# Norm sums of the last two channel blocks in one accumulation group per PSUM bank, with later identity products and a halved first output piece

## The chip, the cores and the metric

The kernel runs on one core of a Trainium2 chip. The metric is the device time of one execution in microseconds (us); lower is better.

## The reference

One inference step through one layer of a decoder trunk, for a prompt of 256 tokens and for 8 samples of one token each, with `D_MODEL = 2048`. What matters here is the end of each of its two sub-layers: an output projection, a root-mean-square norm over the 2048 channels of each token, and a residual sum.

```python
def rmsnorm(x, g):
    xf = x.astype(jnp.float32)
    y = xf * lax.rsqrt(jnp.mean(xf * xf, axis=-1, keepdims=True) + EPS)
    return (y * g.astype(jnp.float32)).astype(x.dtype)

def trunk(x, c, s_hg, s_gla, p):
    # ... three token mixers, merged by gates ...
    out = merged @ p['w_out'][l]                                          # 2048 -> 2048
    x = x + gt1 * rmsnorm(out, p['g_post_mix'][l])
    h2 = rmsnorm(x, p['g_pre_mlp'][l]) * (1.0 + sc2) + sh2
    y2 = jnp.square(jax.nn.relu(h2 @ p['w_mlp_up'][l])) @ p['w_mlp_down'][l]  # 2048 -> 8192 -> 2048
    x = x + gt2 * rmsnorm(y2, p['g_post_mlp'][l])
```

The results are `y_prompt` (256 tokens by 2048 channels), `y_sample` (8 by 2048), the states of two recurrences and one set of gate rows.

## The kernel before

**Layout and products.** Activations are kept with channels on the 128 partitions and tokens along the free axis: 256 prompt tokens and 8 samples, 264 columns. Every large weight is streamed from HBM in tiles, split into a rounded part `whi` (on ScalarE) and a remainder `wlo` (on VectorE), and multiplied in three products per tile (lines 603 to 605). These products fill nearly the whole program. `w_out` and `w_mlp_down` give 16 output blocks of 128 channels each. Blocks 0 to 13 are made in pairs; the last two, 14 and 15, are made one after the other by code of their own, so that work on block 14 can run while TensorE multiplies for block 15.

**The norm sums.** For each block the squares of its 264 columns are added into `sqacc` (128 partitions by 264). The sum over the partitions is a product with ones on TensorE. For the prompt, the 128 columns of a token half `t` are the stationary operand and one column of ones moves, which leaves one sum per token on the partitions, in column `t` of a PSUM tile `ps`; for the samples, the ones are stationary and 8 columns move, which leaves their sums in columns 2 to 9. The squares of block 15 are not added to `sqacc`: they stay in `sq[:, 1, :]`, and each sum is a group of two products, one with `sqacc` and one with `sq[:, 1, :]`. This stands twice: after `w_out` (lines 1672 to 1676) and after `w_mlp_down` (lines 1941 to 1945). Squares and sums are in float32, and each float32 product shows in the trace as two passes on TensorE.

**After `w_out`.** From `ps` come the factors `r1` (a square root on ScalarE, line 1684, and a Newton step on VectorE, lines 1687 to 1695), then those of the next norm, `r2`, then two sets of scaled identity matrices (lines 1718 to 1722), and with these the first input blocks of `w_mlp_up` (`first_quad`, line 1750). While ScalarE and VectorE do this, TensorE works off 40 products of the conditioning matrix (`rounds.steps`, lines 1681 and 1699, the products at line 338).

**After `w_mlp_down`, the tail.** `rstd_sqrt` (lines 190 to 199) makes `r3` from `ps`: one square root on ScalarE and five short operations on VectorE. The output `y = x1 + r3 * yt` has 8 pieces of 128 tokens by 512 channels (`put`, line 1962). VectorE makes five of them (line 1968), and SyncE (SP) issues their transfers. TensorE makes the three in `by_pe`: an identity product that puts `x1` into PSUM (`first_part`, line 1926) and a product with a diagonal matrix of `r3` that adds the scaled rows (line 1973); ScalarE copies the sum out (line 1966) and issues the transfer itself. `rows_tile(1)` (line 1921) turns block 15 to token rows, which ScalarE then copies (line 1953). GpSimd scales the sample rows (lines 1959 and 1960), TensorE transposes them (line 1976), ScalarE copies them (line 1986) and SP issues the last transfer (line 1987).

The order of work on TensorE, VectorE and ScalarE is the order in which the code is written in these two places (`tc.manual_schedule`), so a line moved in the source is moved on its engine. The small PSUM tiles come from a pool of three buffers (`sm`).

## Time and profile before

| | |
|---|---|
| Runs | 1922.57, 4265.69 and 1923.81 us, median 1923.81 |
| Profiled execution | 1922.67 us, of which the span of the instructions is 1920.9 us |
| TensorE clock granted in it | 0.997 of full |
| TensorE busy | 1898.7 us in 17108 instructions |
| VectorE, ScalarE, GpSimd busy | 1201.5, 1007.6 and 156.8 us |
| HBM traffic | 435.99 MB read, 11.70 MB written |

The profile gives, for one execution, when each instruction began, how long it took, what ended the idle time before it, and which chain of work ended last. PE is TensorE's matmul, PEld its weight load, DVE is VectorE, ACT ScalarE, POOL GpSimd; SPq and ACTq are the queues from which SP and ScalarE issue transfers. Times count from the start of the span. A row of the timeline has start, duration, engine, line, operation, the names of output and inputs, shapes and a count of merged instructions; in brackets stand the idle time before it and what ended it.

### The profile page before, as it was taken

How to read it: one execution, taken by the hardware profiler on the slowest of the kernel's cores; microseconds unless marked ns; L12 is line 12 of the kernel's file. 1: busy time of each engine (PE TensorE's matmuls, PEld its weight loads, DVE VectorE, ACT ScalarE, POOL GpSimd, SP SyncE). 2: the span in 40 equal slices, each digit the busy share in tenths (PEclk: the TensorE clock that was granted, in tenths of full speed). 3: DMA queues.
4: the chain of work that ended last, by engine and by line, in shares of the span. 5: the costliest groups of instructions: out<-in, count | busy, mean ns of one | idle time of the engine just before them, and what ended most of it. 6: DMA issues, size and time to landing. Idle time of an engine off the chain costs nothing.

```text
span 1920.9 us, 42626 instructions
## 1 busy us (share of the span) xinstructions
PE 1898.7 (99%) x17108; PEld 1811.6 (94%) x17108; DVE 1201.5 (63%) x2139; ACT 1007.6 (52%) x1821; POOL 156.8 (8%) x314
## 2 busy tenths in 40 slices
PE   7999999999999999999999999999999999999998
PEld 5899999989999999999999989999999999999997
DVE  5666567685576694555555666555766666665666
ACT  4444454655755764544444565555555545454544
POOL 1000000100100101000000010121212121210000
PEclk8999999999999999999999999999999999999999
DMA  9996686776776777767787846797867776866553
GB/s 330 342 329 244 227 304 207 230 230 201 224 244 199 227 233 249 243 205 251 255 265 230 295 146 188 253 306 221 250 211 246 222 250 214 251 206 187 182 180 107
DMA packets 342455, 450.48 MB, mean 235 GB/s; under 512 B 15522, under 2 KB 281520, under 8 KB 342256
## 3 DMA queue, kind: packets, MB, share of 16 engines
q1 hardware_dynamic: 330000, 409.95, 66.2%
q0 software_dynamic: 11648, 36.94, 6.1%
q8 instruction: 134, 2.20, 0.5%
q10 hardware_dynamic: 608, 0.86, 0.1%
q14 instruction: 65, 0.53, 0.1%
HBM read 435.99 MB, written 11.70 MB: 233 GB/s over the span
## 4 chain that ended last, share of the span: by engine, by line
PE 97%; DMA 2%; DVE 1%; ACT 1%; issue 0%; SPq 0%; ACTq 0%
PE mm L603 29%; PE mm L604 29%; PE mm L605 29%; PE ada L338 3%; PE ada L270 1%; PE sm L653 1%; DMA raw<-in_w_in_dram 1%; PE sm L887 1%; DMA b<-in_w_ada_dram 1%; PE sm L660 1%; DVE wlo L107 0%; DMA b<-in_x_prompt_dram 0%; PE sm L994 0%; PE sm L1340 0%; PE sm L1295 0%; PE sm L1320 0%
## 5 line engine op out<-in xcount | busy, mean ns | idle before, releaser
L603 PE MATMUL mm<-b,whi 128*128 128x264 f32 x4568 | 1310.1, 287 | 4.3 <-DVE b L859 1.9
L604 PE MATMUL mm<-b,whi 128*128 128x264 f32 x4568 | 1298.9, 284 | 1.0 <-DVE b L107 0.9
L605 PE MATMUL mm<-b,wlo 128*128 128x264 f32 x4568 | 1296.4, 284 | 0.0
L107 DVE TENSOR_TENSOR wlo<-raw,whi 128x512 fp32r<-128x512 f32 x1136 | 775.4, 690 | 517.1 <-ACT whi L110 513.1
L110 ACT CAST whi<-raw 128x512 fp32r<-128x512 f32 x1132 | 696.3, 618 | 736.2 <-PE mm L604 672.6
L603 PEld LDWEIGHTS mm<-b,whi 128*128 128x128 f32 x4568 | 859.2, 188 | 46.2 <-issue 28.6
L604 PEld LDWEIGHTS mm<-b,whi 128*128 128x128 f32 x4568 | 859.8, 188 | 1.7 <-DVE b L107 0.7
L605 PEld LDWEIGHTS mm<-b,wlo 128*128 128x128 f32 x4568 | 859.3, 188 | 0.0
L104 DVE TENSOR_TENSOR b<-b,mm 128x528 f32<-128x528 f32 (+1 forms) x137 | 95.8, 700 | 95.0 <-PE mm L605 92.5
L1383 ACT ACTIVATE st<-st,sx 128x128 f32<-128x128 f32 (+1 forms) x96 | 39.2, 433 | 37.3 <-POOL sx L1380 37.3
L1384 DVE SCALAR_TENSOR_TENSOR st<-vbc,sx,st 128x128 f32<-128x128 f32 (+1 forms) x96 | 36.1, 394 | 28.8 <-ACT st L1383 28.8
L1362 POOL COPY sa<-vt 128x1 f32<-128x1 f32 x24 | 16.8, 699 | 297.4 <-ACT vt L1828 297.4
L338 PE MATMUL ada<-araw,cT 128*32 128x512 f32 x296 | 40.3, 601 | 0.0
L270 PE MATMUL ada<-b,cT 128*32 128x256 f32 (+1 forms) x640 | 34.6, 352 | 3.4 <-ACT b L234 2.7
L101 DVE TENSOR_TENSOR b<-b,b 128x512 f32<-128x512 f32 (+1 forms) x47 | 33.9, 741 | 1.7 <-ACT b L1262 0.9
L1362 POOL COPY sa<-b 128x1 f32<-128x1 f32 x42 | 18.9, 451 | 178.5 <-DVE b L104 142.0
L270 PEld LDWEIGHTS ada<-b,cT 128*32 128x32 f32 x640 | 17.8, 113 | 15.2 <-DMA b<-in_w_ada_dram 3.4
L338 PE MATMUL ada<-b,cT 128*32 128x512 f32 x216 | 25.8, 593 | 0.0
L107 DVE TENSOR_TENSOR b<-gt,b 128x528 fp32r<-128x528 f32 x32 | 22.7, 708 | 3.3
L107 DVE TENSOR_TENSOR b<-b 128x1024 f32<-128x1024 f32 (+1 forms) x24 | 24.3, 1016 | 0.0
L1367 POOL DMA_DIRECT2D out_dram<-st x32 | 23.6, 738 | 2.6 <-issue 2.6
L101 DVE TENSOR_TENSOR gt<-vt 128x528 f32<-128x528 f32 x32 | 22.4, 701 | 0.9 <-ACT vt L1828 0.9
(428 smaller groups left out, 1003.6 us busy)
## 6 DMA issues: line engine op xcount, KB each, us to landing
raw<-in_w_in_dram SPq DMA_DIRECT2D x231, 512.0 KB, 4.2
raw<-in_w_mlp_up_dram SPq DMA_DIRECT2D x128, 512.0 KB, 4.1
raw<-in_w_mlp_down_dram SPq DMA_DIRECT2D x128, 512.0 KB, 4.4
b<-in_w_ada_dram SPq DMA_DIRECT2D x102, 512.0 KB, 6.5
araw<-in_w_ada_dram SPq DMA_DIRECT2D x74, 512.0 KB, 5.4
raw<-in_w_branch_dram SPq DMA_DIRECT2D x48, 512.0 KB, 4.0
raw<-in_w_out_dram SPq DMA_DIRECT2D x32, 512.0 KB, 4.2
b<-in_w_ada_dram SPq DMA_DIRECT2D x32, 256.0 KB, 5.5
```

The lines of the kernel that those rows point to most:

```text
L101: V.tensor_tensor(o, a, b, op=ALU.mult)
L104: V.tensor_tensor(o, a, b, op=ALU.add)
L107: V.tensor_tensor(o, a, b, op=ALU.subtract)
L110: S.copy(hi, src)
L270: T.matmul(acc[32 * j:32 * j + 32, 0:n], cT[:, k, :], w[:, n * j:n * j + n], start=k == 0, stop=k == KT - 1)
L338: T.matmul(self.acc[32 * j:32 * j + 32, :], cT[:, k, :], ws[j // 2][:, j % 2 * 512:j % 2 * 512 + 512], start=k == 0, stop=k == KT - 1)
L603: T.matmul(o, a, xh(k + j), start=first and j == 0, stop=False)
L604: T.matmul(o, a, xl(k + j), start=False, stop=False)
L605: T.matmul(o, b, xh(k + j), start=False, stop=last and j == n - 1)
L1362: nc.gpsimd.tensor_copy(tmp([P, 16], "sa")[:, 0:1], paced[0])
L1383: S.activation(st[:, i, :], st[:, i, :], AF.Copy, scale=fk[:, 0, j:j + 1])
L1384: V.scalar_tensor_tensor(st[:, i, :], v[:, i, :], fk[:, 1, j:j + 1], st[:, i, :], ALU.mult, ALU.add)
```

## The change

A helper `norm_products(ps, v, first)` makes the three sums for one set of squares. It is called once with `sqacc` and once with the squares of block 15. Only the very first product starts an accumulation group, and all later ones, which go to other columns of the same PSUM tile, are written as going on with it. The call for `sqacc` stands ahead of `gated_tile(1)`, in which the squares of block 15 are made; the call for those squares stands behind it. This is done after `w_out` and after `w_mlp_down`.

In the tail, the identity products of the first two TensorE pieces now stand behind `rows_tile(1)`, the third in the loop ahead of its own diagonal product. The first VectorE piece is worked out and transferred as two halves of 256 channels.

```diff
+    def norm_products(ps, v, first):
+
+        for t in range(2):
+            T.matmul(ps[:, t:t + 1], v[:, t * P:(t + 1) * P], ones[:, 0:1], start=first and t == 0, stop=not first, skip_group_check=True)
+        T.matmul(ps[:, 2:2 + NS], ones, v[:, NP:NT], start=False, stop=not first, skip_group_check=True)
...
     tile_products(1, got[1], 12)
     ps = sm([P, 2 + NS])
+    norm_products(ps, sqacc, True)
     gated_tile(1)
-    for t in range(2):
-        for i, v in enumerate((sqacc, sq[:, 1, :])):
-            T.matmul(ps[:, t:t + 1], v[:, t * P:(t + 1) * P], ones[:, 0:1], start=i == 0, stop=i == 1)
-    for i, v in enumerate((sqacc, sq[:, 1, :])):
-        T.matmul(ps[:, 2:2 + NS], ones, v[:, NP:NT], start=i == 0, stop=i == 1)
+    norm_products(ps, sq[:, 1, :], False)
...
     last_products(1, 1)
-    first_part(0)
+    ps = sm([P, 2 + NS])
+    norm_products(ps, sqacc, True)
     gated_tile(1)
-    ps = sm([P, 2 + NS])
-    for t in range(2):
-        for i, v in enumerate((sqacc, sq[:, 1, :])):
-            T.matmul(ps[:, t:t + 1], v[:, t * P:(t + 1) * P], ones[:, 0:1], start=i == 0, stop=i == 1)
-    for i, v in enumerate((sqacc, sq[:, 1, :])):
-        T.matmul(ps[:, 2:2 + NS], ones, v[:, NP:NT], start=i == 0, stop=i == 1)
+    norm_products(ps, sq[:, 1, :], False)
     r3 = tmp([P, 2 + NS], "nr", 1)
     rstd_sqrt(ps, 1.0 / D, r3)
     rows_tile(1)
+    first_part(0)
     first_part(1)
-    first_part(2)
...
-        y = piece(yt, *p)
-        if p in by_pe:
-            S.copy(y, sums_pe[p])
-        else:
-            V.scalar_tensor_tensor(y, y, r3[:, t:t + 1], piece(x1, *p), ALU.mult, ALU.add)
-        eng = nc.scalar if p in by_pe else nc.sync
-        eng.dma_start(y_prompt[0, t * P:(t + 1) * P, hf * 1024 + c0:hf * 1024 + c0 + 512], y)
+        y, x = piece(yt, *p), piece(x1, *p)
+        n = 256 if p == (0, 0, 0) else 512
+        for c in range(0, 512, n):
+            if p in by_pe:
+                S.copy(y, sums_pe[p])
+            else:
+                V.scalar_tensor_tensor(y[:, c:c + n], y[:, c:c + n], r3[:, t:t + 1], x[:, c:c + n], ALU.mult, ALU.add)
+            eng = nc.scalar if p in by_pe else nc.sync
+            d0 = hf * 1024 + c0 + c
+            eng.dma_start(y_prompt[0, t * P:(t + 1) * P, d0:d0 + n], y[:, c:c + n])
 
     for i, p in enumerate(by_pe):
+        if i == 2:
+            first_part(2)
```

The lines below are rows of the built program in their order on one engine, with line, operation, output and inputs, size of the output, and the semaphores for which an instruction waits. Line numbers in the changed kernel are some lines off: the sums are at lines 210 and 211 there.

First, TensorE after `w_out`, from the first sum to the transposes of block 15. `a` is `sqacc`, `vt` the squares of block 15, `cst` the ones, `gt` the block to be transposed. Before:

```order
L1674 MATMUL sm_14758<-cst,a_2211_13478 128x1 [waits DVE_49]
L1674 MATMUL sm_14758<-cst,vt_14682 128x1 [waits Activation_49]
L1674 MATMUL sm_14758<-cst,a_2211_13478 128x1
L1674 MATMUL sm_14758<-cst,vt_14682 128x1
L1676 MATMUL sm_14758<-a_2211_13478,cst 128x8
L1676 MATMUL sm_14758<-vt_14682,cst 128x8
L1633 MATMUL sm_14770<-cst,gt_14683 128x128 [waits DVE_49,PE_49]
L1633 MATMUL sm_14771<-cst,gt_14683 128x128 [waits PE_49]
```

The same place in the changed kernel:

```order
L210 MATMUL sm_14758<-cst,a_2211_13478 128x1 [waits DVE_49]
L210 MATMUL sm_14758<-cst,a_2211_13478 128x1
L211 MATMUL sm_14758<-a_2211_13478,cst 128x8
L210 MATMUL sm_14758<-cst,vt_14682 128x1 [waits Activation_49]
L210 MATMUL sm_14758<-cst,vt_14682 128x1
L211 MATMUL sm_14758<-vt_14682,cst 128x8
L1639 MATMUL sm_14770<-cst,gt_14683 128x128 [waits DVE_49,PE_49]
L1639 MATMUL sm_14771<-cst,gt_14683 128x128 [waits PE_49]
```

The product that waits for ScalarE's squares was the second of six and is now the fourth; behind it stand two more sums instead of four.

Second, TensorE in the tail, from the end of the products of block 15. Line 1926 (1929 in the changed kernel) is an identity product, line 1921 (1924) a transpose of block 15. Before:

```order
L1926 MATMUL mm_24805<-b_13471,cst 128x512 [waits DMASW5_49]
L1943 MATMUL sm_24877<-cst,a_2211_13478 128x1 [waits DVE_49]
L1943 MATMUL sm_24877<-cst,vt_24807 128x1 [waits Activation_49]
L1943 MATMUL sm_24877<-cst,a_2211_13478 128x1
L1943 MATMUL sm_24877<-cst,vt_24807 128x1
L1945 MATMUL sm_24877<-a_2211_13478,cst 128x8
L1945 MATMUL sm_24877<-vt_24807,cst 128x8
L1921 MATMUL sm_24857<-cst,gt_24808 128x128 [waits DVE_49]
L1921 MATMUL sm_24857<-cst,gt_24808 128x128
```

Now:

```order
L210 MATMUL sm_24872<-cst,a_2211_13478 128x1 [waits DVE_49]
L210 MATMUL sm_24872<-cst,a_2211_13478 128x1
L211 MATMUL sm_24872<-a_2211_13478,cst 128x8
L210 MATMUL sm_24872<-cst,vt_24807 128x1 [waits Activation_49]
L210 MATMUL sm_24872<-cst,vt_24807 128x1
L211 MATMUL sm_24872<-vt_24807,cst 128x8
L1924 MATMUL sm_24857<-cst,gt_24808 128x128 [waits DVE_49]
L1924 MATMUL sm_24857<-cst,gt_24808 128x128
```

The identity product that stood ahead of the sums is gone from here, and the three sums of `sqacc` stand in its place.

Third, what follows on TensorE up to the end: line 1973 (1977) is a diagonal product, line 1976 (1980) the transpose of the sample rows, which waits for GpSimd. Before:

```order
L1926 MATMUL mm_24806<-b_13473,cst 128x512 [waits DMASW7_49]
L1926 MATMUL sm_24896<-b_13472,cst 128x512 [waits PE_49]
L1973 MATMUL mm_24805<-b_24228,vt_24900 128x512 [waits Activation_49]
L1973 MATMUL mm_24806<-b_24230,vt_24900 128x512 [waits Activation_49]
L1976 MATMUL sm_24908<-cst,sqs_24903 128x128 [waits DVE_49,Pool_49]
L1973 MATMUL sm_24896<-b_24229,vt_24900 128x512
```

Now:

```order
L1929 MATMUL mm_24805<-b_13471,cst 128x512 [waits DMASW5_49]
L1929 MATMUL mm_24806<-b_13473,cst 128x512 [waits DMASW7_49]
L1977 MATMUL mm_24805<-b_24228,vt_24898 128x512 [waits Activation_49]
L1977 MATMUL mm_24806<-b_24230,vt_24898 128x512 [waits Activation_49]
L1980 MATMUL sm_24906<-cst,sqs_24901 128x128 [waits PE_49,Pool_49]
L1929 MATMUL sm_24908<-b_13472,cst 128x512 [waits DVE_49]
L1977 MATMUL sm_24908<-b_24229,vt_24898 128x512
```

Two identity products still stand ahead of the diagonal products; the third has gone behind the transpose of the sample rows. On the queues, ScalarE's third output transfer now also waits for the transfer of the first half piece, whose semaphore it uses again; before, only the transfer of the sample rows waited in this way, for the first whole piece.

## The prediction

> **What bounds the kernel now.** I read the page first, for the engine that is full.

> ```profile
> span 1920.9 us, 42626 instructions
> PE 1898.7 (99%) x17108; PEld 1811.6 (94%) x17108; DVE 1201.5 (63%) x2139; ACT 1007.6 (52%) x1821; POOL 156.8 (8%) x314
> PE 97%; DMA 2%; DVE 1%; ACT 1%; issue 0%; SPq 0%; ACTq 0%
> ```

> The third line is the chain that ended last: 97% of the span is TensorE. The change leaves the large products alone, so it can only touch the two places where TensorE stands at the end of a short serial chain: the norm after `w_out` (about 1131 us) and the tail (from 1907 us). There I read the timeline. After `w_out`:

> ```profile
> 1131.16 0.28 PE L1674 MATMUL sm<-cst,a 128*128 128x1 f32 x2
> 1131.54 0.41 ACT L1625 ACTIVATE vt<-mm 128x264 f32<-128x264 f32 x1
> 1132.00 0.38 PE L1674 MATMUL sm<-cst,vt 128*128 128x1 f32 x2 [0.57 <-ACT vt L1625]
> 1132.25 0.36 PE L1674 MATMUL sm<-cst,a 128*128 128x1 f32 x2
> 1132.47 0.36 PE L1674 MATMUL sm<-cst,vt 128*128 128x1 f32 x2
> 1132.69 0.37 PE L1676 MATMUL sm<-a,cst 128*128 128x8 f32 x2
> 1132.92 0.37 PE L1676 MATMUL sm<-vt,cst 128*128 128x8 f32 x2
> 1133.38 0.27 ACT L1684 ACTIVATE nr<-sm,eps 128x10 f32<-128x10 f32 x1 [1.43 <-PE sm L1676]
> ```

> Each row is one float32 sum (two passes). TensorE makes one sum of the old squares, stands idle for 0.57 us until ScalarE's squares are there (1131.95), and then needs five sums, 0.22 to 0.25 us from start to start, before the square root may begin. Two of the five, at 1132.25 and 1132.69, use only `a`. The tail shows the same figure:

> ```profile
> 1907.51 1.02 PE L1926 MATMUL mm<-b,cst 128*128 128x512 f32 x2
> 1908.18 0.43 ACT L1915 ACTIVATE vt<-b 128x264 f32<-128x264 f32 x1 [2.85 <-DVE b L104]
> 1908.37 0.28 PE L1943 MATMUL sm<-cst,a 128*128 128x1 f32 x2
> 1908.66 0.38 PE L1943 MATMUL sm<-cst,vt 128*128 128x1 f32 x2
> 1909.57 0.37 PE L1945 MATMUL sm<-vt,cst 128*128 128x8 f32 x2
> 1909.98 0.27 ACT L194 ACTIVATE nr<-sm,eps 128x10 f32<-128x10 f32 x1 [1.37 <-PE sm L1945]
> 1911.01 0.17 DVE L199 SCALAR_TENSOR_TENSOR nr<-sa,nr 128x10 f32<-128x10 f32 x1
> 1911.22 3.78 DVE L1968 SCALAR_TENSOR_TENSOR b<-b,nr,b 128x512 f32<-128x512 f32 x5
> ```

> The identity product fills the wait, and `r3` is ready at 1911.18. What comes after it I read from the transfers, in 40 slices of 0.25 us from 1911 on, and from the rows that issue them:

> ```profile
> GB/s 0 0 0 0 0 0 0 188 418 401 49 401 410 385 393 401 328 360 410 402 426 393 401 344 270 328 393 418 402 373 260 111 18 0 0 0 0 0 0 0
> 1912.00 0.36 SPq L1970 DMA_DIRECT2D out_dram<-b  x1
> 1912.89 0.36 SPq L1970 DMA_DIRECT2D out_dram<-b  x1
> 1913.51 0.35 ACTq L1970 DMA_DIRECT2D out_dram<-b  x1
> 1914.91 0.58 ACT L1966 COPY b<-sm 128x512 f32<-128x512 f32 x1 [0.42 <-PE sm L1973]
> 1915.53 0.34 ACTq L1970 DMA_DIRECT2D out_dram<-b  x1
> 1916.20 0.33 SPq L1987 DMA_DIRECT2D out_dram<-xsn  x1
> out_dram<-xsn SPq DMA_DIRECT2D x1, 64.0 KB, 3.7
> DMA to landing us min/median/max: 2.2/3.0/4.0
> ```

> The first piece, issued at 1912.00, moves from about 1912.85; there is a hole in the slice at 1913.5; with the second piece, issued at 1912.89, the traffic rises again at 1913.75 and stays near 400 GB/s to about 1918.4. So **the tail ends on a transfer backlog that begins with the second piece**: from then on every piece waits for bandwidth, not for its engine. The last transfer lands 3.7 us after its issue, at 1919.9, where an unhindered piece takes 2.2.

> **The change, part by part.** *Sums after `w_out`.* Three sums of `a` fit into the wait: the first starts at 1131.16, three take about 0.7 us, and the squares come at 1131.95. Behind them stand three sums instead of five: two starts of 0.22 us less, **-0.45 us** at the square root. It reaches the end only if everything behind moves too. The next rows of the chain, and the engines beside it, are:

> ```profile
> 1133.70 4.43 PE ada L338 x40
> 1138.13 0.42 PE sm L1760 x2
> 1138.06 0.30 PEld L1760 LDWEIGHTS sm<-gt,b 128*128 128x128 f32 x2 [0.84 <-ACT gt L1719]
> SPq L557 <- DVE wlo L107: 53.6, 19, 7.3
> ```

> TensorE's 40 conditioning products follow the sums without a gap, and the scaled identities that end its next wait come from the square root through VectorE and ScalarE. Both start from the same sums, so both come 0.45 us earlier. Weight loads wait for VectorE (last row, from 1120 to 1200 us), hence move as well. I see nothing that is late in their place, and TensorE sets the time from there to 1907 us, so I take the whole 0.45; bounds 0 (another wait absorbs it) and -0.50 (two starts of 0.25).

> *Sums in the tail.* The three sums of `a` take the identity product's place at 1907.51 and are done by about 1908.3 (0.7 us), before the squares (1908.61). Three sums remain, so the square root starts at 1909.53 instead of 1909.98 and `r3` is ready at 1910.73: **-0.45 us** again. The moved identity product gains nothing itself, since the sums waited for ScalarE. That the sums share one accumulation group costs nothing: first and later products of a sum have the same rows (0.36 to 0.38).

> *Identity products.* Two still stand between the transposes and the diagonal products, 0.86 us each; the cover is the wait for `r3`. In the chain:

> ```profile
> 1911.07 0.86 PE sm L1926 x2
> 1911.93 0.94 PE mm L1973 x2
> 1913.66 1.02 PE L1973 MATMUL sm<-b,vt 128*128 128x512 f32 x2
> ```

> The diagonal product starts when the second identity product ends, 1911.93, now 1911.48, so the first two pieces come 0.45 us earlier. The third is late: an identity product of 0.86 us now stands directly ahead of its diagonal product, which ended at 1914.68 and now ends at 1914.68 - 0.45 + 0.86 = 1915.09. ScalarE, which was free at 1914.9, copies about 0.2 us later. Behind that copy stand the issue of its transfer, the copy of the sample rows and SP's last transfer: issues at 1915.75 and 1916.42 instead of 1915.53 and 1916.20. Their data can move from about 0.9 us after that, 1916.6 and 1917.3, while the backlog lasts to about 1918.1 even when it ends earlier. So I cost the delay at nothing; without this cover it is +0.22 us, and +0.51 if the two products don't overlap at all (two rows of 1.02 in place of 0.86 each, and the sample transpose before them).

> *First piece in halves.* No row shows 128x256 in this operation. The nearest are:

> ```profile
> 1905.10 0.44 DVE L104 TENSOR_TENSOR a<-a,vt 128x264 f32<-128x264 f32 x1
> L1968 DVE SCALAR_TENSOR_TENSOR b<-b,nr,b x5: 739/753/940, 1911.2 to 1914.3; 128x512 f32<-128x512 f32 x5
> ```

> Two of 0.43 against one of 0.75 make the four pieces behind 0.1 us later; bounds 0 (no cost of its own) and 0.17 (a whole 128x10 operation, the row at 1911.01). I take 0.1. The first bytes leave 0.45 + 0.33 us earlier, but the backlog still begins with the second whole piece, and for that only -0.45 + 0.10 = **-0.35 us** counts. Each half holds 128 KB, 0.33 us at 400 GB/s; even at half that rate both are gone when the second piece comes (1913.4). SP issues one transfer more (0.36 us), inside its waits for VectorE. ScalarE's third transfer now waits for the first half to land, 1911.2 + 2.2 = 1913.4, two us before its turn; behind it in ScalarE's queue stands only the copy of the sample rows.

> [...]

> The sum: -0.45 - 0.35 = -0.80 us on the profiled execution's 1922.67, **1921.9 us**. That execution lies 1.14 us below the median shown (1923.81) and 0.10 above the lowest run.

> **The rivals.**

> *The late third piece sets the end.* If the last transfer lands a fixed 3.7 us after its issue, because the end hangs on its own chain and not on the backlog, the tail pays +0.22 instead of gaining 0.35: 1922.67 - 0.45 + 0.22 = 1922.4, at most 1922.7. For it: that transfer is the last to be issued and to land. Against it: 3.7 against 2.2 us for an unhindered piece.

> *The change doesn't do what it says after `w_out`.* The earlier square root meets another wait between 1133 and 1150 us and the 0.45 is lost; the tail's remains: 1922.3. Against it: both paths start from the sums.

> *Slower: TensorE's clock falls.* In the tail TensorE now stands idle from about 1908.3 to 1908.66, where the identity product was. If that halved the clock, the products after it, some 6 us up to 1914.7, would take 12: the third piece's sum is ready near 1921, its copy, issue and landing take another 4, and the end lies about 5 us later, 1922.67 - 0.45 + 4.7 = 1926.9. It decides from the idle time at which the clock gives way. The rows:

> ```profile
> 1917.00:1918.00 1.00, 0.00 (x0) 0.00 (x0) 0.00 (x0) 0.00 (x0) 0.00 (x0) 1.00 1.02 352
> 1918.00:1919.00 1.00, 0.00 (x0) 0.00 (x0) 0.00 (x0) 0.00 (x0) 0.00 (x0) 0.79 0.80 286
> 1131.00:1134.00 3.00, 2.43 (x23) 2.09 (x25) 1.56 (x10) 1.49 (x8) 0.00 (x0) 1.00 0.00 0
> ```

> (The last three columns: granted clock, DMA share, GB/s.) After the last product (1914.7) the clock is full for over 3 us, and in the stretch with 0.57 us of idle it stays 1.00. [...]

> **How the numbers follow.** The forecast, 1921.9: 0.60. Late third piece, 1922.4: 0.20. Nothing gained after `w_out`, 1922.3: 0.14. Clock, 1926.9: 0.02. The other 0.04 is for disturbed executions, of which the runs before show one at 4265.69, and for what I don't foresee. Bounds on the effect are -0.50 - 0.45 = -0.95 and +0.51, so 1921.7 to 1923.2 for an execution like the profiled one. The two ordinary runs before differ by 1.24 us, more than the effect, and the profiled one is near their lower end; I add that spread on both sides: **1920.5 to 1924.4**. About 2% of the time, 38 us, is what a measurement can tell from no change; none of the named cases comes near, and only the last 0.04 can lie outside: faster 0.01, same 0.97, slower 0.02.

> **What would show it.** Right: three sums of `a` before ScalarE's squares in both places, idle ahead of the fourth; square root 0.45 us sooner after the squares; first transfer issued 0.75 to 0.8 us sooner after them; no hole in the traffic after the second whole piece; the last landing about 0.35 us earlier against the end of block 15's products. Wrong: the third piece's copy more than 0.5 us later, traffic that sags before the sample rows move, a granted clock below 1.00 before 1914 us, or sums that take longer in one shared group.

## Result and profile after

The changed kernel takes 1920.72 us in the median of 22 runs (1919.56 to 1922.88), the kernel before, run beside it, 1923.07 (21 runs from 1921.03 to 1925.59, and the one of 4265.69): a ratio of 0.9986, 95% interval 0.998 to 0.9992. That is 2.7 us faster, between 1.5 and 3.8 (2.35 by the two medians). By the bound of 2% it is no change, but it is no scatter either: two more copies of it, in another series, gave 0.9987 [0.9978, 0.9996] and 0.9988 [0.9979, 0.9997]. The forecast was 1921.9 us, 0.80 us faster. The measured time lies inside its range, near the lower end, which is wide because of the spread of the runs; the change itself is about three times the forecast's.

The profiled execution after took 1922.71 us, one of the slowest of its 22, and its span equals that of before:

```profile
span 1920.9 us, 42630 instructions
PE 1900.0 (99%) x17108; PEld 1812.7 (94%) x17108; DVE 1202.0 (63%) x2140; ACT 1007.3 (52%) x1821; POOL 155.9 (8%) x314
PE 97%; DMA 2%; DVE 1%; ACT 0%; issue 0%; SPq 0%; ACTq 0%
```

So the two totals tell nothing of the change, and the stages have to be laid against an instruction that both kernels have. After `w_out`, the timeline of the kernel after (start, duration, engine, line, operation; in brackets the idle time before it):

```profile
1131.52 0.28 PE L1604 MATMUL mm<-b,wlo 128*128 128x264 f32 x1
1131.64 0.50 PE L210 MATMUL sm<-cst,a 128*128 128x1 f32 x4
1132.00 0.37 PE L211 MATMUL sm<-a,cst 128*128 128x8 f32 x2
1132.03 0.41 ACT L1631 ACTIVATE vt<-mm 128x264 f32<-128x264 f32 x1
1132.49 0.61 PE L210 MATMUL sm<-cst,vt 128*128 128x1 f32 x4
1133.43 0.27 ACT L1687 ACTIVATE nr<-sm,eps 128x10 f32<-128x10 f32 x1 [0.98 <-PE sm L211]
```

All three sums of `a` are now made before ScalarE's squares are there. From the last `w_out` product (1131.52) to the square root it takes 1.91 us; before it took 1133.38 - 1131.04 = 2.34. Nearly all of these 0.43 us is kept: from that product to the last product of block 15 it takes 775.97 us, before 776.35 (0.38 less; 0.45 over the profiles in the table below).

The tail, from the same view:

```profile
1907.49 0.28 PE L1909 MATMUL mm<-b,wlo 128*128 128x264 f32 x1
1907.62 0.50 PE L210 MATMUL sm<-cst,a 128*128 128x1 f32 x4
1908.28 0.42 ACT L1918 ACTIVATE vt<-b 128x264 f32<-128x264 f32 x1 [2.85 <-DVE b L104]
1908.76 0.61 PE L210 MATMUL sm<-cst,vt 128*128 128x1 f32 x4 [0.41 <-ACT vt L1918]
1909.63 0.27 ACT L194 ACTIVATE nr<-sm,eps 128x10 f32<-128x10 f32 x1 [0.93 <-PE sm L211]
1910.67 0.17 DVE L199 SCALAR_TENSOR_TENSOR nr<-sa,nr 128x10 f32<-128x10 f32 x1
1910.88 4.01 DVE L1969 SCALAR_TENSOR_TENSOR b<-b,nr,b 128x256 f32<-128x256 f32 x6
1910.94 0.42 POOL L1958 TENSOR_TENSOR os<-os,nr 128x128 f32<-128x128 f32 x1 [179.22 <-DVE nr L199]
1911.44 0.53 POOL L1959 TENSOR_TENSOR sqs<-os,xsT 128x128 f32<-128x128 f32 x1
1911.67 3.58 SPq L1972 DMA_DIRECT2D out_dram<-b  x6
```

The square root starts 1.35 us after the squares began (before 1909.98 - 1908.18 = 1.80): 0.45 us sooner. The first transfer is issued 3.39 us after the squares (before 3.82), only 0.43 us sooner and not 0.75 to 0.8, because the first half piece took as long as a whole one. The six pieces by duration (minimum, median, maximum in ns), and below them the traffic in 40 slices of 0.25 us from 1911 on:

```profile
L1969 DVE SCALAR_TENSOR_TENSOR b<-b,nr,b x6: 672/739/765, 1910.9 to 1914.2; 128x512 f32<-128x512 f32 x4, 128x256 f32<-128x256 f32 x2
```

```profile
GB/s 0 0 0 0 0 0 274 250 135 361 29 287 393 402 393 393 369 336 418 393 385 418 360 311 312 369 401 402 402 371 318 146 55 4 0 0 0 0 0 0
```

The two halves are the 672 and the 765. The hole stands at 1913.5 as before; from the second whole piece on (1913.75) the traffic sags no deeper than before (lowest slice 311 GB/s, before 270, until it runs out). The second piece (whole in both kernels; the prediction calls it the second whole piece) is issued 5.48 us after the start of the last product of block 15, before 5.49, so the backlog begins no earlier. The last landing comes 12.46 us after that start, the same as before.

### The profile page after: what moved, and what is told of

Same layout as the page of the kernel before. It is cut to its first block, busy times and chain, and to the rows that moved or that the text cites. A ratio compares the mean times of both kernels' runs of the same rounds, so it can differ in the third digit from the quotient of the medians.

```text
span 1920.9 us, 42630 instructions
## 1 busy us (share of the span) xinstructions
PE 1900.0 (99%) x17108; PEld 1812.7 (94%) x17108; DVE 1202.0 (63%) x2140; ACT 1007.3 (52%) x1821; POOL 155.9 (8%) x314
## 4 chain that ended last, share of the span: by engine, by line
PE 97%; DMA 2%; DVE 1%; ACT 0%; issue 0%; SPq 0%; ACTq 0%
PE mm L609 29%; PE mm L610 29%; PE mm L611 29%; PE ada L344 3%; PE ada L276 1%; PE sm L659 1%; DMA raw<-in_w_in_dram 1%; DMA b<-in_w_ada_dram 1%; PE sm L893 1%; PE sm L666 1%; DVE wlo L107 0%; DMA b<-in_x_prompt_dram 0%; DVE b L104 0%; PE sm L1000 0%; PE sm L1346 0%; PE sm L1326 0%
## 5 line engine op out<-in xcount | busy, mean ns | idle before, releaser
L107 DVE TENSOR_TENSOR wlo<-raw,whi 128x512 fp32r<-128x512 f32 x1136 | 776.0, 690 | 517.7 <-ACT whi L110 513.0
L104 DVE TENSOR_TENSOR b<-b,mm 128x528 f32<-128x528 f32 (+1 forms) x137 | 95.8, 699 | 95.0 <-PE mm L611 92.5
L107 DVE TENSOR_TENSOR b<-gt,b 128x528 fp32r<-128x528 f32 x32 | 22.7, 709 | 3.3
L107 DVE TENSOR_TENSOR b<-b 128x1024 f32<-128x1024 f32 (+1 forms) x24 | 24.4, 1022 | 0.0
```

The lines of the kernel that those rows point to most:

```text
L104: V.tensor_tensor(o, a, b, op=ALU.add)
L107: V.tensor_tensor(o, a, b, op=ALU.subtract)
```

## The experiments

Times are medians with the runs of the kernel before from the same series beside them; where means are given, one standard error stands behind ±. Two theories were open. **Stage sum**: the change is worth what its two stages show, 0.45 + 0.25 us. **Clock**: something that only some executions show, and that this change takes away, is worth the rest.

**The change taken apart.** Eight kernels: the kernel before itself, only the sums after `w_out`, only the sums and identity products of the tail, only the halves, the kernel after twice, the kernel after with the first piece whole, and the kernel after with GpSimd's work in the tail put ahead of `r3`.

```
e2  before, with     norm_products(ps, sqacc, True); gated_tile(1); norm_products(ps, sq[:, 1, :], False)   (after w_out only)
e3  before, with     the same in the tail, first_part behind it; first piece whole
e4  before, with     n = 256 if p == (0, 0, 0) else 512
e7  after,  with     n = 512
e8  after,  with     ys = gs + xsT ahead of r3 on GpSimd, and   - Q.tensor_tensor(gs, gs, r3s...)
```

The kernel e8 leaves the factor `r3` out of the sample rows.

> The kernel before, unchanged, measured against itself. The measured change (ratio 0.9986, about 2.7 us) is larger than the 0.8 us of the forecast. Theory 'terms' (the gain is real and sits in the changed places): ratio 1.000, within 0.0004. Theory 'scatter' (stretches that the change does not touch differ from program run to program run): this ratio may be off 1 by 0.0005 or more, and the profile differs from the one of before by 0.5 to 1.2 us ahead of 1131 us.

> Only the sums after w_out are regrouped. Both theories: in the profile the square root there comes 0.4 to 0.45 us sooner after ScalarE's squares, and what follows keeps it; the tail is as before. 'Terms': time -0.45 us if my term is right, -1.5 to -2 us if the larger gain sits here. 'Scatter': -0.45 us give or take 1.

> Only the tail's sums are regrouped and the identity products moved; the first piece stays whole. If the halves cost what they bring: the second piece is issued 0.45 us sooner after the last product than before (5.5 us there), the last landing 0.3 to 0.45 us sooner, time -0.3 to -0.45 us. If the late third piece sets the end: +0.2 us. If the larger gain sits in the tail: -1.5 us or more.

> Only the first output piece is made and sent in two halves. My term: +0.1 us (backlog begins 0.1 us later). If a half costs VectorE nearly as much as a whole piece while GpSimd works beside it (0.77 and 0.67 us in the changed kernel): the second whole piece is issued 0.4 to 0.6 us later than before, and the last landing is 0.3 to 0.5 us later. If the early start of the traffic is what counts: 0.3 us faster.

> The changed kernel again. The changed stretches of the profiles so far add up to about 0.7 us (0.45 after w_out, 0.25 in the tail, with the halves near 0). Theory 'scatter' (the rest of the measured 2.7 us comes from the first 40 us, whose length differed by 3 us between six profiles of the same code there): ratio near 0.9996, -0.7 us give or take 1.5. Theory 'terms' (the changed kernel really is 2.7 us faster): 0.9986 again.

> The same file as e5_after, on the same chip in the same call, as a measure of what two such results can differ by. 'Scatter': the two differ by up to 1 us, and their profiles begin the products after w_out at times that differ by 0.5 to 3 us. 'Terms': both 0.9986, and the same stages.

> The change without the halves (both sums regrouped, identity products moved, first piece whole). If halves bring nothing: within 0.2 us of e5_after, last landing 12.2 to 12.4 us after the last product, as in the kernel with the tail's sums alone (12.34) and the changed kernel (12.46). If halves bring what my forecast's first bytes suggest: 0.3 us slower than e5_after.

> The changed kernel with GpSimd's work moved ahead of r3: the sample rows are summed without their norm factor, so y_sample leaves that factor out; nothing else is left out. If GpSimd beside VectorE is what makes halves dear: each half takes 0.40 to 0.45 us instead of 0.77 and 0.67, the second whole piece is issued near 4.9 us after the last product instead of 5.48, and the last landing comes 0.3 to 0.5 us sooner (12.0 instead of 12.46). If a half simply costs that much: halves as in the changed kernel.

| kernel | median, us | ratio to before, interval | last `w_out` product to last product of block 15 | from there to the end |
|---|---|---|---|---|
| e1, before | 1923.48 | 1.000 [0.9991, 1.0008] | 776.42 | 13.81 |
| e2, `w_out` sums | 1923.15 | 0.9997 [0.9988, 1.0006] | 775.94 | 13.62 |
| e3, tail | 1922.05 | 0.9994 [0.9985, 1.0003] | 776.42 | 13.38 |
| e4, halves | 1922.74 | 0.9999 [0.999, 1.0008] | 776.38 | 13.79 |
| e5, after | 1921.25 | 0.9987 [0.9978, 0.9996] | 775.96 | 13.39 |
| e6, after | 1921.22 | 0.9988 [0.9979, 0.9997] | 775.93 | 13.38 |
| e7, first piece whole | 1921.78 | 0.9991 [0.9982, 1.0] | 775.95 | 13.22 |
| e8, GpSimd ahead | 1920.40 | 0.9987 [0.9979, 0.9996] | 775.94 | 12.91 |

The kernel before had 1923.05 beside e1 to e4 and 1923.45 beside e5 to e8. By the intervals only e5, e6 and e8 differ from it; what e2, e3 and e4 do to the total is within the noise, and only their stages can be read.

The fourth column is as sharp as one could wish: 776.4 with the old order, 775.95 with the new. The last column scatters with the old tail (13.5 to 13.8), for a reason that the traces show: beside GpSimd VectorE's first piece takes either 0.75 us (the profile of before) or 1.03 (e1), and the second piece is issued 5.49 or 5.79 us after the last product of block 15. With the new tail and the first piece whole both come 0.45 us sooner: 5.04 in e7 and 5.35 in e3. The column says that the halves bring nothing, and the pieces say where the time for them goes: with halves (e5, e6) it is issued after 5.48. VectorE's pieces in e8 and in e7:

```profile
L1968 DVE SCALAR_TENSOR_TENSOR b<-b,nr,b x6: 478/743/744, 1909.1 to 1911.9; 128x512 f32<-128x512 f32 x4, 128x256 f32<-128x256 f32 x2
```

```profile
L1967 DVE SCALAR_TENSOR_TENSOR b<-b,nr,b x5: 739/751/943, 1910.8 to 1913.8; 128x512 f32<-128x512 f32 x5
```

With nothing on GpSimd a half takes 0.48 us, and the end comes 0.5 us sooner (12.91). With GpSimd beside it a half takes up to 0.77 and a whole piece up to 0.94 (1.03 in e1): the halves were hindered, not split in cost. But the single parts do not sum up to the -2.2 of e5 and e6, and 2.2 is three times what the stages show.

**The executions above 1924.** The list of single runs had a hint: kernels with the old order after `w_out` had runs at 1924 to 1926, those with the new order none. So the next kernels work on TensorE's wait there: filled with products that nobody reads (e9), kept while the tail is changed (e10), made longer (e11), and the kernel before profiled once more (e12).

```
e9   before   tile_products(1, got[1], 12)
            + for j in range(4):
            +     T.matmul(zb[:, 1, 0:NT], got[1][j // 2][0][:, j % 2, P:2 * P], mH(12 + j), start=True, stop=True)
e10  after, with the loops of before instead of the two norm_products after w_out
e11  before + S.activation(sq[:, 1, :], zt[1], AF.Square)      ahead of gated_tile(1) after w_out
```

> The kernel before with four extra products of 128x264 (0.12 us each, into a bank that nothing reads) put into TensorE's 0.57-us wait behind the last w_out product, ahead of the first `a` sum; the order of the sums is that of before, and nothing is removed. Stage sum alone: nothing gained, up to 0.05 lost; the time is that of before (about 1923.1), with executions at 1924 to 1926 as often as there. Rival (the clock is granted at half for one window of 3.4 us behind that wait in a part of the executions, which costs about 2 us each time): no idle spell, so no execution above 1924, median 1921.5 to 1922.2.

> The kernel after with the sums of the last w_out blocks as before: only the tail's part of the change. Stage sum alone: 1923.1 - 0.25 = 1922.8, and executions at 1924 to 1926 as in before. Rival (idle spell in the w_out stage sets a slower clock in a part of the executions): the same 1922.8 or so, since that wait is there; a second rival, that the tail holds what the executions above 1924 lose: 1921.4, none above 1923.5.

> The kernel before with ScalarE's squares of the last w_out block made twice (0.41 us), so that TensorE's wait behind the last w_out product grows from 0.57 to 0.98 us. Stage sum alone: 1923.1 + 0.41 = 1923.5. Rival (the clock at half for a window behind that wait): the wait is longer, so more executions fall under it: 1924.5 to 1925.5, and rows with a granted clock of 0.5 near 1132 to 1136 us.

> The kernel before, unchanged, profiled once more, to see one of its executions above 1924. Stage sum alone: 2.34 us from the last w_out product to the square root and 776.4 to the last product of block 15, whatever the total. Rival (half clock behind the idle spell): if the total is above 1924, one of the two stretches is 1.5 to 2 us longer, with a granted clock of 0.5 in it.

Measured: before 1922.98; e9 1922.77 (1920.73 to 1923.47), e10 1923.14 (up to 1924.78), e11 1924.67 (up to 1925.49), e12 1924.07 (one run). The intervals of e9, e10 and e11 against the kernel before all hold 1 (e11: 0.9997 to 1.0015), so the profiles have to decide. Three of them show a window of half clock behind that wait: those of e10, e11 and e12 (1923.22, 1925.34 and 1924.07 us, so a run can have the window and stay below 1924). In e12, the unchanged kernel, TensorE's timeline and the windows (length, busy time and count of PE, PEld, DVE, ACT, POOL; then granted clock, DMA share, GB/s) are:

```profile
1131.65 0.38 PE L1674 MATMUL sm<-cst,vt 128*128 128x1 f32 x2 [0.55 <-ACT vt L1625]
1133.27 6.20 PE L338 MATMUL ada<-b,cT 128*32 128x512 f32 x40
```

```profile
1130.40:1133.80 3.40, 2.85 (x29) 2.42 (x31) 1.92 (x13) 1.89 (x9) 0.00 (x0) 1.00 0.00 0
1133.80:1137.20 3.40, 3.40 (x24) 0.85 (x20) 2.98 (x19) 2.27 (x8) 1.36 (x3) 0.50 0.01 2
```

In the profile of before the same products and the same stretch of time are:

```profile
1133.63 4.50 PE L338 MATMUL ada<-b,cT 128*32 128x512 f32 x40
```

```profile
1134.00:1138.00 4.00, 4.00 (x40) 1.04 (x32) 3.54 (x21) 2.87 (x9) 1.70 (x4) 1.00 0.36 75
```

The 40 conditioning products behind the sums take 6.20 us instead of 4.50. From 1133.8 to 1137.2 the granted clock is 0.50, and the same product takes

```profile
L338 PE MATMUL ada<-b,cT 128*32 128x512 f32 x24 | 4.5, 906 | 0.0
...
L338 PE MATMUL ada<-b,cT 128*32 128x512 f32 x20 | 2.4, 610 | 0.0
```

906 ns in that window and 610 right behind it (the last two figures of a row: mean ns, idle time before). The path waits for these products: from the last `w_out` product to the first `w_mlp_up` product it takes 12.30 us instead of 10.61, and to the last product of block 15 778.10 instead of 776.35. **Here a window of 3.41 us at half clock costs 1.7 us.** The same stretch of time in e11 and in e9:

```profile
1134.00:1138.00 4.00, 4.00 (x26) 1.65 (x29) 2.99 (x19) 2.63 (x10) 1.35 (x3) 0.57 0.01 2
```

```profile
1134.00:1138.00 4.00, 4.00 (x40) 1.97 (x33) 2.55 (x11) 2.06 (x6) 2.57 (x8) 1.00 0.71 229
```

The longer wait has the half clock (0.57 over 4 us), the filled one doesn't, though its products are all extra work that made the stage 0.3 us longer. So e11 and e12 went as the clock theory has it and against the stage sum alone (1923.5 for e11). e9 has no run above 1924, as the clock theory says, but its median is 0.6 to 1.3 above what was expected for that; 0.3 of this are the products themselves. For e10 both expected the same; the second rival there, that the tail holds what is lost (1921.4, nothing above 1923.5), did not come (1923.14, up to 1924.78).

| profile | weak stretch, us | window that holds most of it | the whole stretch in it? | clock in the next window |
|---|---|---|---|---|
| before | 1131.16 to 1133.63 | 1130.11 to 1133.52 | no, 2.36 us of it | 1.00 |
| e1, e3, e4, e15 (old order) | | a border falls inside the stretch | no | 1.00 |
| e10 (old order) | 1130.10 to 1132.57 | 1129.84 to 1133.25 | yes | 0.50 |
| e12 (old order) | 1130.82 to 1133.27 | 1130.39 to 1133.80 | yes | 0.50 |
| e11 (old order, longer wait) | 1131.66 to 1134.83 | 1130.73 to 1134.14 | no, 2.48 us of it | 0.50 |
| e13 (new order, longer wait) | 1130.40 to 1132.88 | 1130.29 to 1133.70 | yes | 0.50 |
| e6 (after) | 1129.44 to 1131.50 | 1128.87 to 1132.28 | yes | 1.00 |
| e2, e8, e16, e18 (new order) | 2.05 to 2.06 us long | | yes | 1.00 |
| e9 (old order, filled) | 1129.46 to 1132.22 | 1129.32 to 1132.73 | yes | 1.00 |

By this count the profile of before, on which the forecast stood, has a border 0.1 us ahead of the end of the stretch, and its clock stayed at 1.00. If the windows fall anywhere with equal chance and only a whole stretch counts, the old order is hit in (3.41 - 2.47) / 3.41 = 28 of 100 executions (an estimate from these rows). Above 1924 us lie 46 of 179 runs of the kernel before, and none of 132 runs of the kernel after and of the kernels with the new order or a filled wait.

**Bringing it back, and taking the start out.** e13 makes the wait in the changed kernel longer; e14 has the tail's part and a filled wait; e15 and e16 put 14 products into another wait of TensorE, at 32 to 34 us, on the kernels before and after, to take out the scatter of the start.

```
e13  after  + S.activation(sq[:, 1, :], zt[1], AF.Square)      ahead of gated_tile(1) after w_out
e14  e10 with the four products of e9
e15, e16  in granule(), second group of w_in, behind the first accumulator:
            + for _ in range(14):
            +     T.matmul(acc0[:, 1, NT:512], a, xh(k)[:, 0:512 - NT], start=False, stop=False, skip_group_check=True)
```

> The kernel after with ScalarE's squares of the last w_out block made twice (0.41 us), so that TensorE waits there again: about 0.41 us plus what the three older sums left of the wait, and the weak stretch from the last w_out product to the first conditioning product is about as long as in before (2.3 to 2.5 us). Theory (a clock window of 3.41 us that holds too much of that stretch is followed by one at half clock, 1.7 us lost): median 1920.8 + 0.4 = 1921.2, and between a fifth and a half of the executions 1.7 us above that, up to 1924.5. Rival (only the wait of 0.57 us counts, whatever stands behind it): the same stage sum, no execution above 1923.3.

> The tail's part of the change alone, with the w_out sums in the order of before and four products of 0.12 us in TensorE's wait there: no half clock behind that wait. Stage sum: e9 (mean 1922.45) less the 0.25 of the tail: 1922.2. Rival (the tail takes about 1 us that the profiled executions do not show): 1921.3 or less.

> The kernel before with 14 products of 128x248 (0.12 us each, into columns that nothing reads) put into TensorE's wait of 2.3 to 2.8 us at 32 to 34 us of the program, so that the window there is not followed by one at half clock at 35 to 38 us (six of the fourteen profiles have that one; the last w_out product stands 1.4 us later in them on average). Theory: mean 1923.1 - 0.4 x 1.4 = 1922.5, and two groups of executions left, about 1.7 us apart, by the clock behind the w_out wait. Rival (VectorE's evacuations set that stretch, and the clock there costs nothing): 1923.1 as before.

> The kernel after with the same 14 products in the wait at 32 to 34 us. Theory: mean 1921.0 - 0.4 x 1.4 = 1920.4, with the upper executions (above 1921.7) gone; the lowest as in after, 1919.6. Rival (VectorE's evacuations set that stretch): 1921.0, spread as in after. Against the same kernel without the change (the run with the warm start on the kernel before) the difference is then free of the start: 0.7 by the stage sum, 1.2 to 1.6 with a half-clock window in 30 to 50 of 100 executions of that one.

e13: 1922.99 (up to 1925.44), 2.3 us above the first 22 runs of the kernel after for 0.41 us of extra work, and its profile has the window:

```profile
1134.00:1138.00 4.00, 4.00 (x27) 0.92 (x21) 3.10 (x15) 2.52 (x7) 2.33 (x6) 0.61 0.29 60
```

(The half clock began at 1133.70 there.) This is the strongest of the runs: the change is all there, only the weak stretch is as long as before, and the gain is gone (ratio to before 1.0, interval 0.9992 to 1.0009). It is also more than the clock theory asked for: a median of 1921.2 and nothing above 1924.5. Against the mean of the kernel after the loss is 1.9 ± 0.45 us, where 0.41 and 28 windows in 100 executions would make 0.9. e14: mean 1922.25 ± 0.33, as the stage sum said (1922.2); this pair shows no hidden microsecond in the tail. e15 1922.71 (1921.48 to 1925.05) and e16 1921.54 (1921.04 to 1922.16): means 1923.04 ± 0.36 and 1921.52 ± 0.12. Much of the scatter is gone in e16, and six runs of e15 (1921.48 to 1922.71, mean 1922.14) stand 0.6 us above it, which is the stage sum, while the other five (1923.31 to 1925.05, mean 1924.1) stand 2.6 above. That is how the clock theory would part them, but the parting was made afterwards and by the time alone, the groups are 2.0 apart and not 1.7, and the mean clock of the two kernels' runs does not show it (2.04 ± 0.45 and 2.35 ± 0.35 half windows, counted as below). Both kernels took 1.2 us longer than theirs without the extra products between `w_out` and block 15 (777.58 and 777.21), so what the start gave (no half-clock window is left in the first 40 us of the two profiles, and the last `w_out` product comes at 1129.56 and 1129.10 us) was lost again: a miss of the expectation. The two kernels' means are 1.5 ± 0.4 apart, inside the 1.2 to 1.6 that the theory gave.

**Two attempts at a better version.** e17 has 16 products at the start instead of 14; e18 makes the sample rows' scaling on VectorE behind the second whole piece.

```
e18       put((0, 0, 512))
        + V.tensor_tensor(gs, gs, r3s..., op=ALU.mult); V.tensor_tensor(ys..., gs, xsT, op=ALU.add)
        + T.transpose(ps, ys..., ident)
```

> The kernel after with 16 products of 128x248 in TensorE's wait at 32 to 34 us, where the run before had 14. That run was narrow (1921.04 to 1922.16), but the stretch from the last w_out product to the last product of block 15 took 777.2 instead of 775.95: the products of the down projection came at 12.60 us for each granule instead of 12.51. Theory (the place of the later instructions in the stream sets that, and two products more move it back): 1920.3, range 1919.8 to 1921. Rival (extra products at the start cost 1.2 us later whatever their number): 1921.5 again.

> The kernel of the other run of this pair with GpSimd's two operations on the sample rows (0.42 and 0.53 us beside VectorE's first pieces) made on VectorE, behind the second whole piece, and the sample's transpose behind the three identity products. Theory: the two halves and the first whole piece come at 0.48, 0.48 and 0.74 us as in e8, the last landing 0.4 us sooner: 0.4 below the other run. Rival (two operations of about 0.3 us on VectorE put off the pieces behind them and open a hole in the store traffic): the same time or 0.2 more.

e17 1921.56 and e18 1921.15, before 1923.08. The 1.2 us were lost again (777.21 and 777.19), so their cause is not the number of extra products; TensorE waits nowhere longer, and what they are stays open. In e18 the halves and the first whole piece take 0.48, 0.48 and 0.74 us as in e8, but the pieces behind come later, and the last landing (12.42 us after the last product of block 15, e17 12.29) is not earlier. No kernel that makes the whole output is clearly faster than the kernel after (e18's ratio to before is 0.999, those of e5 and e6 0.9987 and 0.9988).

## Why the prediction was right and wrong

**Right, step by step.** Three sums of `a` stand before the squares in both places. The square root comes 0.43 to 0.45 us sooner in both, and the whole of it after `w_out` reaches block 15 (776.4 to 775.95 in all profiles of e1 to e8). The shared accumulation group costs nothing: the sums behind the squares start 0.22 to 0.24 us apart, before 0.22 to 0.25. The third piece on TensorE is late by about the 0.2 us named: SP's last transfer goes out 9.04 us after the last product's start, before 8.80, and the traffic before it sags no deeper than before, so it is hidden as said. The rival that the last transfer sets the end, and the one that nothing is gained after `w_out`, did not come.

**The term of the halves was mis-sized.** "Two of 0.43 against one of 0.75" became 0.77 and 0.67 (0.48 and 0.66, with 0.94 for the piece behind them, in the profiles of e13 and e17), since GpSimd scales the sample rows at that moment (the POOL rows at 1910.94 and 1911.44). GpSimd's rows were in the trace of before too and were not laid beside VectorE's. So at the second piece the halves cost not 0.1 but 0.13 to 0.44 us: it is issued after 5.48 us with them and after 5.04 (e7) or 5.35 (e3) without. Two signs that the prediction named for being right did not come for it: the first transfer was 0.43 us sooner and not 0.75 to 0.8, and the last landing was not sooner than in the profile of before. With nothing on GpSimd beside them both halves take 0.48 us, in e8 and in e18, against the 0.67 and 0.77; by what the two engines hinder each other no run shows. The tail's end came 0.06 us sooner than in the profile of before and about 0.25 sooner than the mean of the old tails (13.61 over seven profiles, 13.38 over eight of the new), instead of 0.35.

**The step that failed** is the one on the clock: the prediction priced TensorE's wait behind `w_out` at its own 0.45 us and put what the clock does behind it at nothing. It named half clock behind a short idle spell as a rival, in the tail, and turned it down because "in the stretch with 0.57 us of idle it stays 1.00". That was one execution, and in it a window border fell inside the stretch (at 1133.52 by the count). The half clock was looked for only where the change might add an idle spell (the tail, which showed 1.00 in every profile before the last product), and not where the change takes one away. e10, e12, e11 and e13 show what stood there: 1.7 us in the executions with about 2.5 us of the stretch in one window; with it the path to block 15 takes 778.1 us instead of 776.4 (e10, e12).

**What that makes of the measured change.** The stages give 0.45 + 0.25 = 0.70. The windows behind `w_out` add, in the mean and as an estimate, 1.7 us in 28 of 100 executions, 0.5, or in 5 of 11, as the runs of e15 may be parted, 0.8. Over the runs whose clock is on record the means of the two kernels are 1923.01 (147 runs) and 1920.99 (44 runs), 2.0 apart. So 0.5 to 0.8 us of these 2.0, and more of the first result's 2.7, are not accounted for.

The clock granted in each run counts the half windows of an execution, (1 - clock) x 1921 / 1.71, since 3.413 us at 0.50 take away 1.71 us at full clock: 2.99 ± 0.12 in the 147 runs of before, 1.74 ± 0.19 in the 44 of after, 3.06 in e11, 3.47 in e13, 1.33 in e9. In runs with a clock of 0.999 or more before stands at 1921.76 (26 runs) and after at 1921.12 (24): 0.64 apart, the stage sum. But the count does not carry the rest: at a clock of 0.998 the two stand at 1922.52 (43 runs) and 1920.64 (8), at 0.997 at 1924.10 (41) and 1920.95 (11), so 1.9 and 3.2 apart with the same number of windows. It also holds windows that cost nothing: behind the last product the clock falls to half as well (0.50 from 1918.58 us on in before, from 1917.40 on in after), and 0.1 to 1.25 windows of a profile lie there inside the span.

Not settled is what the rest is. Two of the seven profiles with the old, unfilled order show the window behind `w_out`, and none shows one elsewhere between 40 us and the end of the products. A rival that no run excludes is the start of the program. When the parts that the profiles give as fixed are taken from a kernel's mean time (the stretch from `w_out` to block 15, the mean of the tail, and the 1.78 us by which the time exceeds the span), the time up to the last `w_out` product is left: 1129.9 us in after, 1130.1 in e8, 1130.4 in e9 and e14, 1130.7 in e7 and 1131.5 in e2 (± 0.1 to 0.3). None of their profiles has the window behind `w_out`, the code up to there is the same, and still they differ by up to 1.6 us. The kernel before, with its windows behind `w_out` still in the figure, has 1131.2. So the start can differ from kernel to kernel by as much as the rest, for a cause that stays open; e2, with the new order and a mean of 1922.86 ± 0.31 where the clock theory asks for 1922.1 or less, is the plainest case. The one pair in which the first 40 us were made alike, e15 and e16, speaks for this rival: it stands 1.5 ± 0.4 apart, which the stages and the windows behind `w_out` cover (0.7 and 0.5 to 0.8). One pair does not prove it.

## What to carry over

Before a microsecond is priced by one trace, several profiles of the same kernel belong side by side, with the granted clock around each idle spell: here a spell that cost its own 0.57 us in one execution (before) cost 1.7 more in another of the same kernel (e12: 12.30 us to the first `w_mlp_up` product instead of 10.61). Work that was due anyway, put into this wait, saved 0.45 us, and in the profiles with it (e2, e6, e8, e16, e18) the clock behind the wait stayed at 1.00. In the profile of e9, with products that nobody reads in the wait, it stayed at 1.00 too, but they cost 0.3 us themselves, and e9 was not clearly faster than the kernel before (ratio 0.9998, interval 0.9989 to 1.0007). And a piece that is halved has to be priced beside what the other engines do in that very microsecond: a half took 0.48 us in e8 and 0.67 and 0.77 beside GpSimd.

## What the hardware showed that was not expected

Half a microsecond of idle time and some 1.9 us of products with 1 to 128 moving columns were followed by half clock over the next 3.41 us (e10, e12, e13); 2.06 us of such a stretch, with 0.12 us of idle time, were not (e6; e2, e8, e16 and e18 alike), nor 2.36 us of the old stretch (before). The first 40 us have half-clock windows at a different place in nearly every profile (none in e6, one at 36 in e7, four from 12 to 40 in e2), and the last `w_out` product comes at 1129.3 to 1132.6 us: 1131.3 in the mean of the seven profiles with a window that begins at 35 to 37 us, 1130.0 in the nine others (before, after and e1 to e14). In the profiles of e15 to e18, with products put into the wait at 32 to 34 us, no such window is left, and it comes at 1128.6 to 1129.7.
